# A decoder layer on one core: both ends laid out anew — the first phase in blocks of 256 tokens by two k-tiles, the last token tiles of 128 rows with the second half of the tokens completed first

## The chip, the cores and the metric

The kernel runs on one core of a Trainium2 chip. A core has five engines: TensorE (PE in the profile; PEld is its weight load), VectorE (DVE), ScalarE (ACT), GpSimd (POOL) and SyncE (SP), and here SP and POOL start the DMAs. The metric is the device time in microseconds of one execution; the figure given is the median of three.

## The reference

One step of a decoder layer on 512 new prompt tokens and 8 sample tokens, all in fp32; the model is 2048 wide. Half of the mixing is a gated delta rule with 8 heads of 128, half a pooling over trailing windows; a SwGLU layer 5632 wide follows, and a final norm.

```python
def decoder_layer(h, conv_buf, S0, pool_buf, start_pos, chunked, ...):
    xn = rmsnorm(h, norm_mix)
    proj = xn @ w_in                      # q | k | v | z | beta | decay | pool
    ...
    qkv_c, new_conv = short_conv(conv_buf, qkv, conv_w)       # 4 taps, then silu
    ...
    q = l2norm(q) * (DN_HEAD_DIM ** -0.5)
    k = l2norm(k)
    beta = sigmoid(b_raw)
    g = -exp(a_log) * softplus(a_raw + dt_bias)
    o, S = gated_delta_chunked(q, k, v, g, beta, S0f)          # samples: token by token
    dn_out = rmsnorm(o, dn_norm) * silu(z)
    pool_out, new_pool = multiscale_pool(pool_buf, p, start_pos, w_pool, pool_scale)
    h = h + concatenate([dn_out, pool_out]) @ w_out
    gu = rmsnorm(h, norm_ffn) @ w_gate_up
    h = h + (silu(gu[..., :D_FF]) * gu[..., D_FF:]) @ w_down
    return h, S, new_conv, new_pool
...
y_prompt = rmsnorm(hp, norm_final)
y_sample = rmsnorm(hs, norm_final)
```

## The kernel before

The 520 tokens (8 samples first, then the prompt) lie along the free dimension, and the 2048 channels as 16 tiles (k-tiles) of 128 partitions: `xh` and `xl` hold the normed input, `mixa` and `mixb` the raw one (8 k-tiles each) and later other things. Every fp32 operand is cut in a high part (`hi`, rounded) and a low part (`lo`, what is left), and each product is three matmuls (`step`, L179 to L181): high weight by high and by low input, low weight by high input. The tokens are worked in two chunks, `CHUNKS`, of 264 (samples and 256 prompt tokens) and 256. A weight tile arrives as granules of 8 k-tiles (`granule`): a DMA on SP into `raw`, the high part on ScalarE (L146), the low part on VectorE (L148).

**First phase** (the pool `ph0`, L265 to L512), written out by hand: the order of the lines is the order on every engine. The prompt arrives as four tiles of 128 tokens (`load_x`), and the work is 16 `Block`s of one token tile by four k-tiles: `turn` transposes it on TensorE to PSUM (L318), `fetch` copies it to `mixa`/`mixb` (L321), `norm` multiplies the copy by norm weight and root, four operations of 128 columns (L326), `high` makes the high part on ScalarE (L330), `low` the low part, mostly on POOL (L333). The root of a token tile comes from square sums (L283, L285), a power on POOL (`pow_mhalf`, L227), a diagonal matrix (L296) and a matmul with ones that spreads it over the partitions (L298). Behind the blocks stand the products of the first two key tiles: `first` in full (2 chunks x 16 k-tiles x 3 matmuls = 96), of `second` the first 8 k-tiles of one chunk (24). At the end the raw input is stored in DRAM (`spill`) on SP.

**The input projection.** Behind it `qkv_tile` makes one tile of 128 columns after the other: `product`, eviction to `ext`, convolution, silu. The tile of head 1 takes over `second` at k-tile 8 of chunk 0: its remaining 72 matmuls stand there. `product` calls `weave.step()` after each k-tile: a planner that lays small work between the matmuls, by steps that are counted; on its second track stand first `gates` (the beta and decay columns), then `keys(h)`, each 16 steps after its tile was made, so a product that is absent here is 16 steps fewer. `gates` stores the cumulative sums of the decays in DRAM (`gcr_d`, a DMA on SP, L617); `decay(h)` reads a head's row back, spread over all partitions (`gcb`, L754), subtracts (L757) and takes the exponential; `keys(h)` makes k times k (L774) and k transposed (L777) in two PSUM banks and scales them on VectorE (L789, L791). The PSUM banks named `dn` are a ring of five (`pst`), those named `mm` one of three.

**The middle** (products of z, q, v, pool, output and gate/up projections) is the same in both kernels, row for row on TensorE.

**The tail.** `w_down` is multiplied in pairs of output tiles by Strassen-Winograd's seven products (`Pair`): raw quarters A11 to A22 are loaded, the sums S1 to S4 made on VectorE (L1246), each cut in high and low (L1217, L1218), and products M1 to M7 accumulate in a `dn` bank each (`multiply`, L1224 to L1226, 24 matmuls here); `combine` adds the results to the residual in `mixa`/`mixb`. The order of the seven is `FIRST` in all pairs, the last too:

```python
    FIRST = ("M1", "M2", "M4", "M7", "M6", "M5", "M3")
```

With it a pair completes its first half of the tokens last. As channels complete, `squares` (L1749) puts their squares into the sum `sq2`. `token_roots` (L1831, L1834) sums `sq2` over the partitions for some token tiles and takes the power on POOL. `tokens(t)` transposes a token tile back (L1846), scales it, half on ScalarE (L1849), half on VectorE (L1851), and stores every 1024 columns by a DMA on SP (L1854, L1856). There are five tiles of `NT` = 104 tokens; the first holds the 8 samples.

## Time and profile before

| | us |
|---|---|
| three runs | 2189.26, 2186.50, 2185.41 |
| median | 2186.50 |
| the profiled execution (one of the three) | 2189.26 |
| its span in the profile | 2187.3 |
| granted clock of TensorE, mean | 0.995 |

The span runs from the first to the last recorded instruction; 1.96 us of the execution's time lie around it. A row of the timeline gives start, duration, engine, line, operation, what it writes and reads, and in brackets how long the engine had been idle and what released it. TensorE's matmuls overlap, so what one costs is read from start to start. Of what the prediction does not show: the DMA engines are used between 20 and 70% in every one of the page's 40 slices.

### The profile page before, as it was taken

To read this page: it belongs to the slowest core of one execution; us is meant where nothing else is said; L and a number is where in the kernel's file an instruction comes from. 1 tells how busy PE (TensorE), PEld (TensorE's weight loads), DVE (VectorE), ACT (ScalarE), POOL (GpSimd) and SP (SyncE) were. 2 spreads that over 40 slices of the span, in tenths; PEclk is the share of its full clock that TensorE was granted. 3 is DMA by queue.
4 is the path that set the end of the run, shared out by engine and by line. 5 is a ranking of instruction groups with operands and counts; after the bars stand their busy time and mean duration, and the time that the engine had idled before them with its cause. 6 is when DMAs were issued, how large, how long until landed. Compare 5 with 4: busy or idle time off the path is not lost.

```text
span 2187.3 us, 42971 instructions
## 1 busy us (share of the span) xinstructions
PE 2143.5 (98%) x17815; PEld 2135.1 (98%) x17815; DVE 1731.4 (79%) x2518; ACT 955.6 (44%) x1491; POOL 465.5 (21%) x520
## 2 busy tenths in 40 slices
PE   5999999999999999999999999999999999999998
PEld 5999999999999999999999999999999999999997
DVE  6576566566489979988888888888877898887996
ACT  5434454343255544443433434434334444445554
POOL 4111011011022211323233233232012303003120
PEclk8999999999999999999999999999999999999999
DMA  6443233423535542545445545554446746337333
GB/s 201 131 103 106 77 89 96 110 68 82 140 103 159 154 137 85 160 138 169 144 142 160 155 138 157 151 151 141 127 145 184 242 110 204 113 109 240 96 106 109
DMA packets 444728, 297.03 MB, mean 136 GB/s; under 512 B 26548, under 2 KB 424653, under 8 KB 441189
## 3 DMA queue, kind: packets, MB, share of 16 engines
q1 hardware_dynamic: 426661, 225.13, 36.6%
q0 software_dynamic: 16880, 68.51, 9.7%
q8 instruction: 139, 2.28, 0.4%
q10 hardware_dynamic: 992, 0.66, 0.1%
q14 instruction: 56, 0.46, 0.1%
HBM read 251.47 MB, written 43.43 MB: 135 GB/s over the span
## 4 chain that ended last, share of the span: by engine, by line
PE 88%; DVE 4%; ACT 2%; issue 1%; DMA 1%; POOL 0%; SPq 0%; DVEq 0%; ACTq 0%; POOLq 0%
PE dn L1224 21%; PE dn L1225 21%; PE dn L1226 21%; PE mm L179 7%; PE mm L181 6%; PE mm L180 6%; DVE lo L1218 1%; PE dn L854 1%; DMA st<-a_d 1%; ACT hi L1217 1%; DVE raw L1246 0%; PE dn L1846 0%; PE dn L964 0%; PE dn L861 0%; PE dn L900 0%
## 5 line engine op out<-in xcount | busy, mean ns | idle before, releaser
L1217 ACT CAST hi<-raw 128x1024 fp32r<-128x1024 f32 (+1 forms) x424 | 429.9, 1028 | 408.6 <-DVE raw L1246 215.0
L1218 DVE TENSOR_TENSOR lo<-raw,hi 128x1024 fp32r<-128x1024 f32 (+1 forms) x424 | 529.5, 1269 | 91.7 <-ACT hi L1217 89.9
L179 PE MATMUL mm<-xh,hi 128*128 128x256 f32 (+1 forms) x1280 | 380.4, 297 | 0.6 <-ACT ccs L735 0.6
L180 PE MATMUL mm<-xl,hi 128*128 128x256 f32 (+1 forms) x1280 | 362.9, 284 | 1.9 <-DVE xl L333 1.8
L181 PE MATMUL mm<-xh,lo 128*128 128x256 f32 (+1 forms) x1280 | 363.2, 284 | 0.2 <-DVE lo L148 0.2
L180 PEld LDWEIGHTS mm<-xl,hi 128*128 128x128 f32 x1280 | 243.7, 190 | 2.3 <-issue 1.9
L179 PEld LDWEIGHTS mm<-xh,hi 128*128 128x128 f32 x1280 | 243.2, 190 | 1.4 <-ACT ccs L735 0.7
L181 PEld LDWEIGHTS mm<-xh,lo 128*128 128x128 f32 x1280 | 242.4, 189 | 0.4 <-DVE lo L148 0.4
L1246 DVE TENSOR_TENSOR raw<-raw 128x1024 f32<-128x1024 f32 (+1 forms) x132 | 177.1, 1342 | 2.2
L1226 PE MATMUL dn<-b21h,lo 128*128 128x260 f32 x628 | 177.9, 283 | 0.1
L1224 PE MATMUL dn<-b21h,hi 128*128 128x260 f32 x628 | 177.7, 283 | 0.0
L1225 PE MATMUL dn<-b21l,hi 128*128 128x260 f32 x628 | 177.3, 282 | 0.4 <-DVE b21l L1730 0.4
L1226 PE MATMUL dn<-b11h,lo 128*128 128x260 f32 x620 | 175.4, 283 | 0.0
L1224 PE MATMUL dn<-b11h,hi 128*128 128x260 f32 x620 | 175.4, 283 | 0.0
L1225 PE MATMUL dn<-b11l,hi 128*128 128x260 f32 x620 | 174.9, 282 | 0.0
L148 DVE TENSOR_TENSOR lo<-raw,hi 128x1024 fp32r<-128x1024 f32 (+1 forms) x86 | 102.6, 1197 | 75.2 <-ACT hi L146 74.9
L1224 PE MATMUL dn<-T1h,hi 128*128 128x260 f32 x564 | 160.2, 284 | 0.0
L1225 PE MATMUL dn<-T1l,hi 128*128 128x260 f32 x564 | 160.0, 284 | 0.0
L1226 PE MATMUL dn<-T1h,lo 128*128 128x260 f32 x564 | 159.0, 282 | 0.0
L1224 PE MATMUL dn<-B22h,hi 128*128 128x260 f32 x556 | 157.6, 283 | 0.0
L1225 PE MATMUL dn<-B22l,hi 128*128 128x260 f32 x556 | 157.2, 283 | 0.0
L1354 POOL TENSOR_TENSOR mixa<-mixa 128x520 f32<-128x520 f32 x22 | 50.8, 2309 | 499.9 <-DVE mixa L1348 499.9
(590 smaller groups left out, 6526.7 us busy)
## 6 DMA issues: line engine op xcount, KB each, us to landing
raw<-in_w_gate_up_dram SPq DMA_DIRECT2D x134, 512.0 KB
raw<-in_w_in_dram SPq DMA_DIRECT2D x80, 512.0 KB
a_d<-mixa POOLq DMA_DIRECT2D x22, 1040.0 KB, 5.5
mixb<-in_w_gate_up_dram SPq DMA_DIRECT2D x42, 512.0 KB
raw<-in_w_down_dram SPq DMA_DIRECT2D x48, 448.0 KB
raw<-in_w_out_dram SPq DMA_DIRECT2D x25, 512.0 KB
st<-a_d POOLq DMA_DIRECT2D x49, 260.0 KB, 6.6
raw<-in_w_down_dram SPq DMA_DIRECT2D x24, 512.0 KB
```

The lines of the kernel that those rows point to most:

```text
L148: dve.tensor_tensor(lo[:, :f], raw[:, :f], hi[:, :f].bitcast(F32), op=ALU.subtract)
L179: te.matmul(acc[ci], wh, hi[k][:, c0:c1], start=(k == 0), stop=False)
L180: te.matmul(acc[ci], wh, lo[k][:, c0:c1], start=False, stop=False)
L181: te.matmul(acc[ci], wl, hi[k][:, c0:c1], start=False, stop=(k == len(w) - 1))
L854: te.matmul(yp[:, ck(c)], xt_[:, ck(c)], cur[:, ck(c)], start=True, stop=True)
L1217: act.copy(hi, raw)
L1218: dve.tensor_tensor(lo, raw, hi.bitcast(F32), op=ALU.subtract)
L1224: te.matmul(acc, wh[:, k, :], xf[:, k, :], start=start and k == 0, stop=False)
L1225: te.matmul(acc, wh[:, k, :], xg[:, k, :], start=False, stop=False)
L1226: te.matmul(acc, wl[:, k, :], xf[:, k, :], start=False, stop=stop and k == wh.shape[1] - 1)
L1246: dve.tensor_tensor(r[name], r[a], r[b], op=op)
L1354: pool.tensor_tensor(q[:, 4:8:2, :], q[:, 1:4:2, :], q[:, 0:2, :], op=ALU.subtract)
```

## The change

**First phase.** A block is now one chunk of 256 prompt tokens (two token tiles) by two k-tiles; 16 of them, those of chunk 0 first. `norm` reads the transposed input out of PSUM instead of the fetched copy, in two operations of 256 columns; all low parts are VectorE's. The loads change order (norm weights, samples and tile 2 ahead of other parameters; weights between tiles 3 and 4), all square sums are made in halves, and a loop over 17 steps does per step: fetch of block i + 2, high part of block i + 1, norm of i + 2, low part of i + 1, transposes of i + 4, and the products of block i. `second` is multiplied in full there too (its last weight granule lies in `hi3`, `lo3`); both key tiles are evicted to `ext` in the phase; the raw input is stored by POOL's queue during the second chunk. `qkv_tile` of heads 0 and 1 has no product left.

**Tail.** The last pair is a `LastPair`: order `LASTLY`, its banks from the ring `mm`, its sums made after the cuts and written over raw quarters, and each half of each output tile squared and scaled where it completes. Token tiles are the four of 128 prompt tokens, the samples are handled by themselves (`sample_rows`). The roots of tiles 2 and 3 and the transposes of tile 2 stand inside the last product M4.

```diff
+    def to_columns(ext, t, ci, acc):
+        if ci == 0:
+            act.copy(ext[:, 3:3 + 256], acc[:, NB:264])
+            act.copy(ccs[:, :, t], acc[:, 0:NB])
+        else:
+            act.copy(ext[:, 3 + 256:3 + 512], acc)
...
+            def norm(self, n=None):
+
+                if not n:
+                    self.xm = ph0.tile([P, 2, 256], F32, name="xm", bufs=4)
+                c = slice(0, 256) if n is None else slice(P * n, P * n + P)
+                r = slice(self.cols.start + c.start, self.cols.start + c.stop)
+                for kk in range(2):
+                    dve.scalar_tensor_tensor(self.xm[:, kk, c], self.pt[:, 256 * kk + c.start:256 * kk + c.stop],
+                                             nmix(self.k + kk), rb[:, r], op0=ALU.mult, op1=ALU.mult)
...
+        load_x(1)
+        sp.dma_start(pr0, norm_mix[0].rearrange("(t p) -> t p", p=P))
+        sp.dma_start(xts[0], x_sample.rearrange("b s (k p) -> (b s k) p", p=P))
+        load_x(2)
+        sp.dma_start(pr1[96:112, :], norm_ffn[0].rearrange("(t p) -> t p", p=P))
+        sp.dma_start(pr1[0:96, :], conv_w[0].rearrange("i (t p) -> (i t) p", p=P))
+        parts[0][0]()
+        load_x(3)
+        parts[1][0]()
+        load_x(4)
+        parts[2][0]()
+        sp.dma_start(wba_raw, w_in[0].rearrange("(k p) c -> p k c", p=P)[:, :, 4096:4112])
+        sp.dma_start(raw3.rearrange("p (k c) -> p k c", k=HG), win_view(1024 + P)[:, HG:2 * HG, :])
...
+            pool.dma_start(xs_d[4 * kg:4 * kg + 4].rearrange("k p c -> p k c"), m[:, r, :])
...
+        for i in range(17):
+            if i + 2 < 16:
+                B[i + 2].fetch()
+            if i + 1 < 16:
+                B[i + 1].high()
+            if i < 4:
+                square_sums(3 + i // 2, act, half[i % 2], i % 2)
+            if i == 1:
+                parts[1][1](act)
+            if i == 3:
+                parts[2][1](act)
+            if i == 6:
+                act.copy(hi3, raw3)
+            if i in (2, 4):
+                roots(2 + i // 2, 2)
+            if i in (4, 6):
+                on_all(1 + i // 2, pbs[1 + i // 2])
+            if i + 2 < 16:
+                B[i + 2].norm()
+            if i + 1 < 16:
+                B[i + 1].low()
+            if i in (2, 4):
+                dgs[2 + i // 2] = diagonal(2 + i // 2)
+                parts[i // 2][1](dve)
+            if i == 6:
+                dve.tensor_tensor(lo3, raw3, hi3.bitcast(F32), op=ALU.subtract)
             if i + 4 < 16:
                 B[i + 4].turn()
+            if i in (3, 5):
+                pbs[(i + 3) // 2] = spread(dgs[(i + 3) // 2])
+            ci, j = divmod(i, 8)
+            if i < 16:
+                first(ci, j)
+            if i == 7:
+                to_columns(ext_first, H, 0, acc_first[0])
+            if i in (9, 11, 13, 15):
+                spill((i - 9) // 2)
+            if 5 <= i < 13:
+                second(0, i - 5)
+            if i == 12:
+                to_columns(ext_second, H + 1, 0, acc_second[0])
+            if i == 15:
+                to_columns(ext_first, H, 1, acc_first[1])
+            if 12 <= i < 16:
+                second(1, i - 12)
+            if i == 16:
+                for j in range(4, 8):
+                    second(1, j)
...
-            if done < KT:
-                product(w or weights(win_view(sec * 1024 + h * P), KT), xhk, xlk, evict, acc, done)
-            else:
-                for ci, (c0, c1) in enumerate(CHUNKS):
-                    evict(ci, c0, c1, acc[ci])
+            if ext is None:
+                ext = columns()
+                product(weights(win_view(sec * 1024 + h * P), KT), xhk, xlk,
+                        lambda ci, c0, c1, acc: to_columns(ext, t, ci, acc))
...
-                         *{0: (w_first, acc_first, KT), 1: (w_second, acc_second, 8)}.get(h, ()))
+                         {0: ext_first, 1: ext_second}.get(h))
...
+    LASTLY = ("M1", "M7", "M6", "M5", "M3", "M2", "M4")
...
+        def take(self):
+            return ps_mm.tile([P, HALF], F32, tag="mm", name="mm")
+
+        def add(self, name):
+            r = self.raw
+            a, b, dst, op = {"S3": ("A11", "A21", "A21", ALU.subtract), "S2": ("A22", "S3", "S3", ALU.subtract),
+                             "S1": ("S2", "A11", "A11", ALU.add), "S4": ("A12", "S2", "S2", ALU.subtract)}[name]
+            r[name] = r[dst]
+            dve.tensor_tensor(r[name], r[a], r[b], op=op)
+
...
+            elif n == "M6":
+                add(u3, p)
+                add(u2, p, m1)
+                add(self.to(1, 1), u3)
+                add(self.to(1, 0), u3)
+            elif n == "M5":
+                add(self.to(1, 1), p)
+                self.done(1, 1)
+                add(u2, p)
+                add(self.to(0, 1), u2)
+            elif n == "M3":
+                add(self.to(0, 1), p)
+                self.done(0, 1)
+            elif n == "M2":
+                add(self.to(0, 0), p)
+                self.done(0, 0)
+            elif n == "M4":
+                add(self.to(1, 0), p)
+                self.done(1, 0)
...
+            lastly = isinstance(p4 or p, LastPair)
+            if name4 in ("S1", "S2", "S3") and not lastly:
                 p4.add(name4)
-            if name and name != "S4":
+            if name and (name != "S4" or lastly):
                 p.cut(name, pool_)
-            if name4 == "S4":
+            if name4 == "S4" or name4[:1] == "S" and lastly:
                 p4.add(name4)
             pairs[q].multiply(n)
             pairs[q].combine(n)
-            if name == "S4":
+            if name == "S4" and not lastly:
                 p.cut(name, pool_)
...
+        def done(i, half):
+
+            m, c = 2 * mp + i, slice(HALF * half, HALF * half + HALF)
+            add_up()
+            sq = wdp.tile([P, NTOK], F32, tag="sq", name="sq")[:, c]
+            act.activation(sq, mix[m][:, c], AF.Square)
+            act.activation(mix[m][:, c], mix[m][:, c], AF.Copy, scale=nfin(m))
+            dve.tensor_tensor(sq2[:, c], sq2[:, c], sq, op=ALU.add)
+
+        if part_ == len(SIZES) - 1 and mp == ORDER[-1]:
+            return LastPair(view, to, done)
...
+        for j in range(n):
+            pow_mhalf(rs[:, j:j + 1], sv[:, j:j + 1])
+            rv[tiles[j] if j < len(tiles) else "s"] = rs[:, j:j + 1]
...
+    def tokens(t, pairs=((2, 3), (1, 0))):
+
+        for pair in pairs:
+            ot = (fins[0][1] if fins else wpl).tile([P, HG * P], F32, tag="ot" if fins else "raw", name="ot")
+            for kg in pair:
+                pt = pst()
+                for kk in range(4):
+                    te.transpose(pt[:, kk * P:(kk + 1) * P], mix[4 * kg + kk][:, tile_(t)], ident)
+                o = ot[:, 512 * (kg % 2):512 * (kg % 2) + 512]
+                if kg % 2 == 0:
+                    act.activation(o, pt, AF.Copy, scale=rv[t])
+                else:
+                    dve.tensor_scalar(o, pt, rv[t], None, op0=ALU.mult)
...
-    def first_half():
-        squares(True)
-        rv.update(token_roots((0, 1)))
-        add_up(dve)
-
-    dps[-1][-1].between["M3"] = first_half
-    run(dps[-1][1:], r21s[1], sums)
+    lastp = dps[-1][-1]
+    lastp.between["M4"] = [(0, lambda: token_roots((2, 3))), (4, lambda: tokens(2))]
+    run(dps[-1][1:], r21s[1], sums, LASTLY)
     stage.pop()[0].close()
     for x in ("T4", "T3", "T2"):
         fls[x].close()
-    fins.append(stacked("fin"))
-    tokens(0, rv[0], (0, 1))
-    squares(True)
-    add_up(dve)
-
-    tokens(0, rv[0], (2, 3))
-    rv.update(token_roots((2, 3, 4)))
-    for t in range(1, 5):
-        tokens(t, rv[t])
+    fins.append(stacked("fin", 6))
+    tokens(3)
+    token_roots((0, 1), True)
+    tokens(0)
+    sample_rows()
+    tokens(1)
```

On ScalarE, in the first phase (`sq` is a square sum, L146 the high part of weights, `mixa`/`mixb` from `dn` a fetch, `xh` from `xm` a high part). Before:

```order
L321 COPY mixa<-dn 128x4x128
L330 CAST xh<-xm 128x4x128
L321 COPY mixb<-dn 128x4x128
L330 CAST xh<-xm 128x4x128
L321 COPY mixb<-dn 128x4x128
L283 ACTIVATE sq_289,ss_128<-xt_135 128x2048
L146 CAST hi<-raw 128x1024
L330 CAST xh<-xm 128x4x128 x2
L449 CAST xh<-xms 128x16x8
L330 CAST xh<-xm 128x4x128
L146 CAST hi<-raw 128x1024
```

After, behind the first high part of weights:

```order
L343 COPY mixa<-dn 128x2x256
L356 CAST xh<-xm 128x2x256
L456 CAST xh<-xms 128x16x8
L343 COPY mixa<-dn 128x2x256 x2
L356 CAST xh<-xm 128x2x256
L300 ACTIVATE sq_264,ss_133<-xt_140 128x1024
L343 COPY mixa<-dn 128x2x256
L356 CAST xh<-xm 128x2x256
L300 ACTIVATE sq_283,ss_133<-xt_140 128x1024
L146 CAST hi<-raw 128x1024
L343 COPY mixb<-dn 128x2x256
L356 CAST xh<-xm 128x2x256
```

Fetches and high parts ran in groups of one to three and square sums over 2048 columns stood between them; now a fetch, a high part and one piece of 1024 columns take turns.

On VectorE, at the first keys of the input projection (`dm` is the decay difference, `gcb` the row read back from DRAM, `kd` and `mixb` what `keys` makes). Before:

```order
L785 TENSOR_TENSOR sck<-sck,btok 128x4
L787 TENSOR_TENSOR sck<-sck,edec 128x4
L791 TENSOR_TENSOR kd<-dn,sck 128x512
L148 TENSOR_TENSOR lo<-raw,hi 128x1024
L757 SCALAR_TENSOR_TENSOR dm<-gcb,gcs,mneg 128x128 x4
L148 TENSOR_TENSOR lo<-raw,hi 128x1024
L757 SCALAR_TENSOR_TENSOR dm<-gcb,gcs,mneg 128x128 x4
L745 TENSOR_SCALAR y<-ext,prm 128x512
L789 SCALAR_TENSOR_TENSOR mixb<-dn,sck,dm 128x128 x8
```

After:

```order
L627 COPY gr<-dn 8x512
L620 TENSOR_SCALAR negc<-negc 128x32
L634 TENSOR_TENSOR sc_g_743<-sc_aq,ident 8x128
L640 COPY sgb<-dn 128x128
L148 TENSOR_TENSOR lo<-raw,hi 128x1024
L744 TENSOR_SCALAR y<-ext,prm 128x512
L779 TENSOR_SCALAR ss<-ss 128x4
L746 SCALAR_TENSOR_TENSOR y<-ext,prm,y 128x512
L756 SCALAR_TENSOR_TENSOR dm<-gcb,gcs,mneg 128x128 x4
L783 TENSOR_TENSOR sck<-rr 128x4
L785 TENSOR_TENSOR sck<-ss,rr 128x4
L746 SCALAR_TENSOR_TENSOR y<-ext,prm,y 128x512
```

The cumulative sums that are stored, `gr`, stand 22 rows ahead of the first `dm` before, with both first keys' `kd` between them; now they stand 8 rows ahead of it, and the first key's results (`mixb` by L788, `kd` by L790) follow it within ten rows.

On TensorE, the end of the last pair (`B22` the tokens' side of M3, `T4` that of M4; `sq` and `sqs` the sums of squares; `ident` marks transposes). Before, the end of the last product M3 and what follows:

```order
L1225 MATMUL dn<-B22l,hi 128x260
L1226 MATMUL dn<-B22h,lo 128x260
L1846 MATMUL dn<-ident,mixa 104x128 x8
L1846 MATMUL dn<-ident,mixb 104x128 x8
L1831 MATMUL dn<-ones,sq_23798 104x2 x3
L1846 MATMUL dn<-ident,mixa 104x128 x8
L1846 MATMUL dn<-ident,mixb 104x128 x8
```

After, the middle of the last product M4:

```order
L1226 MATMUL mm<-T4l,hi 128x260
L1227 MATMUL mm<-T4h,lo 128x260
L1925 MATMUL dn<-ident,mixb 128x128 x8
L1925 MATMUL dn<-ident,mixa 128x128 x8
L1225 MATMUL mm<-T4h,hi 128x260
L1226 MATMUL mm<-T4l,hi 128x260
```

and its end:

```order
L1226 MATMUL mm<-T4l,hi 128x260
L1227 MATMUL mm<-T4h,lo 128x260
L1925 MATMUL dn<-ident,mixb 128x128 x8
L1925 MATMUL dn<-ident,mixa 128x128 x8
L1904 MATMUL dn<-ones,sq_23789 128x2 x2
L1909 MATMUL dn<-ones,sqs 128x2
L1925 MATMUL dn<-ident,mixb 128x128 x8
L1925 MATMUL dn<-ident,mixa 128x128 x8
L1939 MATMUL dn<-ident,xs 128x128
L1925 MATMUL dn<-ident,mixb 128x128 x8
```

Before, all transposes stand behind the last product, the roots of tiles 0 and 1 in the middle of M3 and those of the other three behind the first tile's transposes; now the roots of tiles 2 and 3 stand ahead of M4, tile 2's 16 transposes in the middle of it and tile 3's right behind it, and the samples' tile is a transpose of its own.

More of the change, by code (lines that the diff above doesn't have):

```diff
@@ L392, in decoder_kernel @@
-        B[3].turn()
-        B[2].fetch()
+        dve.tensor_copy(prm[:, 96:112], ptp[:, 0:KT])
         sb = ph0.tile([P, P], F32, name="sb", bufs=1)
         dve.tensor_scalar(sb, ones, ss0[:, 0:1], None, op0=ALU.mult)
-        B[0].norm()
-        roots(2)
         pb = pst()
         te.matmul(pb[:, :NB], sb, sel, start=True, stop=True)
+        for h in range(2):
+            act.copy((mixa, mixb)[h][:, :, 0:NB],
+                     pt0[:, 0:P].rearrange("p (b k) -> p k b", k=KT)[:, 8 * h:8 * h + 8, :])
@@ L401, in decoder_kernel @@
         dve.tensor_scalar(rb[:, 0:NB], pb[:, :NB], 1.0 / D, EPS, op0=ALU.mult, op1=ALU.add)
         pow_mhalf(rb[:, 0:NB], rb[:, 0:NB])
-        B[3].fetch()
-        pt0 = pst()
-        te.transpose(pt0[:, 0:P], xts[0], ident)
-        B[4].turn()
-        B[1].norm()
-        B[0].high()
-        for half in range(2):
-            act.copy((mixa, mixb)[half][:, :, 0:NB],
-                     pt0[:, 0:P].rearrange("p (b k) -> p k b", k=KT)[:, 8 * half:8 * half + 8, :])
-        B[5].turn()
@@ L453, in decoder_kernel @@
+        B[0].low()
         dve.tensor_tensor(xl[:, :, 0:NB], xms, xh[:, :, 0:NB].bitcast(F32), op=ALU.subtract)
[L454 to L470 removed]
@@ L471, in decoder_kernel @@
-        B[12].turn()
-        first(0, 4, 8)
-        parts[2][1](act)
-        B[11].fetch()
-        B[9].high()
-        pb4 = spread(4)
-        B[13].turn()
-        B[8].low(pool)
-        parts[2][1](dve)
-        rows(4, pb4)
-        B[9].low(pool)
-        first(0, 8, 12)
-        B[12].fetch()
-        B[13].fetch()
-        first(0, 12, 16)
-        for i in range(10, 19):
-            if i < 16:
-                B[i].norm()
+        B[1].norm(1)
+        parts[0][1](dve, slice(2 * P, HG * P))
@@ L1167, in decoder_kernel @@
         mixed(0, 2)
+    pres.close()
     c1s.close()
```

328 lines of the change are left out of this document (141 added, 187 removed).

## The prediction

> **What bounds the kernel now.** I read the page first, then the list of waits of each engine, then the two ends row by row. Of the page:
>
> ```profile
> PE 2143.5 (98%) x17815; PEld 2135.1 (98%) x17815; DVE 1731.4 (79%) x2518; ACT 955.6 (44%) x1491; POOL 465.5 (21%) x520
> PE   5999999999999999999999999999999999999998
> ```
>
> TensorE is busy in 98% of the span and only the first and the last of the 40 slices fall short. So there are about 44 us to win, and both are at the ends. TensorE's waits once it runs are few:
>
> ```profile
> PE dn L298 <- DVE dg L296: 11.7, 3, 10.5
> PE dn L362 <- DMA pr<-in_conv_w_dram: 6.5, 1, 6.5
> PE dn L774 <- ACT mixb L748: 0.6, 1, 0.6
> ```
>
> (Columns: total wait in us, how often, the longest.) Both large ones belong to the first phase. Behind it nothing waits long, so what is saved at the head should travel through the dense middle to the end: the order of TensorE's rows is the same there in both kernels.
>
> **The first phase.** Rows of TensorE, then three stretches (busy us of PE, PEld, DVE, ACT, POOL, granted clock, DMA share, GB/s):
>
> ```profile
> 28.26 0.57 PE L179 MATMUL mm<-xh,hi 128*128 128x264 f32 x1
> 55.97 0.39 PE L179 MATMUL mm<-xh,hi 128*128 128x256 f32 x1 [0.58 <-ACT ccs L735]
> 8.00:10.00 2.00, 1.54 (x9) 1.14 (x7) 1.01 (x5) 1.11 (x3) 0.56 (x1) 1.00 0.98 383
> 20.00:25.00 5.00, 0.00 (x0) 0.00 (x0) 4.96 (x16) 2.20 (x5) 1.54 (x2) 0.54 0.41 96
> 38.00:40.00 2.00, 2.00 (x11) 2.00 (x10) 2.00 (x7) 0.00 (x0) 0.48 (x1) 0.50 0.59 227
> ```
>
> The first matmul of a product starts at 28.26 although the loads ran at 383 GB/s by 8; in 20 to 25 VectorE is busy 4.96 of 5 us and TensorE not at all. The prices:
>
> ```profile
> 37.21 0.28 PE L180 MATMUL mm<-xl,hi 128*128 128x264 f32 x1
> 37.33 0.28 PE L181 MATMUL mm<-xh,lo 128*128 128x264 f32 x1
> 38.07 0.42 PE L179 MATMUL mm<-xh,hi 128*128 128x264 f32 x1
> 38.29 0.42 PE L180 MATMUL mm<-xl,hi 128*128 128x264 f32 x1
> 40.92 0.28 PE L180 MATMUL mm<-xl,hi 128*128 128x264 f32 x1
> 36.65 0.60 PE L318 MATMUL dn<-ident,xt 128*128 128x128 f32 x4
> 37.01 0.37 PE L179 MATMUL mm<-xh,hi 128*128 128x264 f32 x1
> 5.65 1.06 ACT L283 ACTIVATE sq<-xt 128x1024 bf16<-128x1024 f32 x1 [3.55 <-DMA xt<-in_x_prompt_dram]
> 34.18 1.06 ACT L146 CAST hi<-raw 128x1024 fp32r<-128x1024 f32 x1
> 35.13 0.60 ACT L321 COPY mixa<-dn 128x512 f32<-128x512 f32 x1
> 35.60 0.64 ACT L330 CAST xh<-xm 128x512 fp32r<-128x512 f32 x1
> 36.12 0.61 ACT L321 COPY mixb<-dn 128x512 f32<-128x512 f32 x1
> 23.45 1.13 DVE L326 SCALAR_TENSOR_TENSOR xm<-mixb,prm,rb 128x128 f32<-128x128 f32 x4
> 17.12 3.15 DVE L326 SCALAR_TENSOR_TENSOR xm<-mixa,prm,rb 128x128 f32<-128x128 f32 x4 [0.98 <-POOL xl L333]
> 30.83 0.68 DVE L333 TENSOR_TENSOR xl<-xm,xh 128x512 fp32r<-128x512 f32 x1
> 80.77 0.75 DVE L747 SCALAR_TENSOR_TENSOR y<-ext,prm,y 128x512 f32<-128x512 f32 x1
> ```
>
> From start to start a product matmul costs 0.12 at full clock (37.21 to 37.33), 0.22 at half (38.07 to 38.29), and four transposes 0.36 (36.65 to 37.01). ScalarE pays 0.95 for 1024 columns (34.18 to 35.13), 0.47 to fetch 512 and 0.52 for their high part. On VectorE four norms of 128 columns take 1.13 alone and 3.15 while POOL subtracts. The new norms are of 256 columns out of PSUM, which no row shows: between 0.28 (1.13 / 4) and the 0.75 of a row of 512 columns I take 0.42, two to a block, 0.83, and 0.61 for the low part. With all low parts on VectorE, POOL has no long work left beside them, so the 3.15 should not recur.
>
> When would the product begin? x of tile 1 has landed by 5.65. Behind it come some 0.07 MB of samples, 1.05 MB of tile 2 and 0.52 MB of weights; at 383 GB/s they are there at about 9 and 10.5. The squares of tile 2 (halves on two engines, about 1.1) end at 10.1. Root, diagonal, spreading, norm and high part follow, about 4.9 with the hand-overs, and the first weights' high cut (0.95) lies among them: 15.0, against 28.26. The order of ScalarE's rows shows the block then being worked as fetch, high part, fetch.
>
> Blocks 0 to 4 are ScalarE's: two copies a block, 1.0, four half squares and three weight cuts of 0.95 among them, and with its waits on VectorE I count 2.6 a block: 15.0 + 5 x 2.6 = 28.0. Then TensorE has 192 - 30 = 162 product matmuls left, 162 x 0.12 = 19.4, and 11 times four transposes, 4.0: 51.4, with 0.3 for the evictions 51.7. VectorE needs 11 x 1.45 + 2 x 1.2 = 18.4 there and stays under it. Two stretches above were granted about half the clock, one with TensorE idle (0.54), one with it busy throughout (0.50); blocks 0 to 4 keep it near half busy, so I add 0.8 (eight matmuls x 0.10): end 52.5. Before, 72 of the 192 matmuls are still to come at 55.97: 72 x 0.12 = 8.6, equal work is done at 64.6. **Gain 12.1**, less 0.25 for the transposes of the parameters now at the phase's end. Bounds: 51 with no cold stretch; 57 where a norm out of PSUM costs 0.67, nearly the row of 512 columns (16 x 2 x 0.25 = 8 more on VectorE, of which about 5 would show).
>
> The Trainium skill (TensorE: Matmul & The Clock Gate, "Part 1: The HAM clock gate") says that TensorE falls to half rate after an idle window of about 3.4 us and comes back after as long a busy one. The row at 0.54, of an idle stretch, agrees. By that rule alone one return, not eight matmuls, would be paid: an estimate of 16 x 0.10 = 1.6.
>
> **The keys.** With 72 matmuls and 16 steps of weaving gone from the second key's tile, the chain of the gates moves against the keys' own rows:
>
> ```profile
> 85.11 0.97 PE dn L614 x8
> 86.82 0.30 SPq L617 DMA_DIRECT2D gcr_d<-gr  x1
> 102.83 0.53 SPq L754 DMA_DIRECT2D gcb<-gcr_d  x1
> 107.88 1.14 DVE L757 SCALAR_TENSOR_TENSOR dm<-gcb,gcs,mneg 128x128 f32<-128x128 f32 x4 [2.10 <-DMA gcb<-gcr_d]
> 109.34 2.15 DVE L789 SCALAR_TENSOR_TENSOR mixb<-dn,sck,dm 128x128 f32<-128x128 f32 x8
> 116.95 1.16 PE dn L774 x8
> ```
>
> Before, 32 us lie between the cumulative sums (85.11) and the last keys (116.95), and the round trip through DRAM (sums, store at 86.82; load at 102.83, landing before 107.88, 4.96 later) hides in them. Now the sums stand directly ahead of keys 0 to 2. Let X be the time of the sums: store at X + 1.7, load landing at X + 8 to 9.5, decay differences 1.14, exponential, then four of the eight rows at 109.34: key 0 leaves its PSUM bank at about X + 13. TensorE has only the sums (0.97), 48 product matmuls (5.8) and some two and a half keys (1.1 to 1.2 each, 3) to do until key 2, whose second bank is the one that key 0 still holds in the ring of five: it is there at about X + 10. So TensorE waits about 3.2 where it waited 0.6 (the row of L774 above): **-2.6**. Behind it queue the next tile's matmuls, and nothing else. Bounds: 0 (the store lands early) and 5 (the load two microseconds later, as its landings scatter).
>
> **The tail.** The last rows:
>
> ```profile
> 2140.00:2150.00 10.00, 10.00 (x86) 10.00 (x85) 9.24 (x14) 5.58 (x8) 0.00 (x0) 1.00 0.28 77
> 2165.60 1.18 POOL L227 TENSOR_TENSOR rv<-sv,mhalf 104x2 f32<-104x2 f32 x1 [33.12 <-DVE sv L1834]
> 2166.70 1.04 PE L1846 MATMUL dn<-ident,mixa 128*104 128x128 f32 x8
> 2167.40 0.69 ACT L1849 ACTIVATE ot<-dn,rv 104x512 f32<-104x512 f32 x1 [2.07 <-PE dn L1846]
> 2172.48 5.05 DVE L1851 TENSOR_SCALAR ot<-dn,rv 104x512 f32<-104x512 f32 x6 [0.19 <-PE dn L1846]
> 2170.00 11.79 SPq L1856 DMA_DIRECT2D out_dram<-ot  x9
> 2178.00:2179.00 1.00, 0.00 (x0) 0.00 (x0) 0.00 (x0) 0.00 (x0) 0.00 (x0) 1.00 0.85 307
> 2185.00:2186.00 1.00, 0.00 (x0) 0.00 (x0) 0.00 (x0) 0.00 (x0) 0.00 (x0) 0.50 0.23 94
> ```
>
> After 2178 every engine is done and only the store runs, at a share of 0.85 and 307 GB/s, until about 2185.35; the span ends 1.95 later. In the change the last pair starts at the same place and has the same seven blocks. I add 16 transposes of tile 2 inside its last block (two of the 1.04 rows overlapping, 1.75) and 1.4 for the squares of the half that completes late, which the roots at that block's head need: its last matmul ends at 2169.8 instead of 2166.7. Behind it stand three prompt tiles of four evictions each on two engines (0.69, and 5.05 / 6 = 0.84), three roots of 1.18 one after the other on POOL, the samples' 128 x 128: the last eviction ends near 2178.6. What is moved out earlier is tile 2's megabyte and half of tile 3's, so the store no longer queues; the last 0.52 MB needs 0.6 to start, 1.7 to move at 307 GB/s with 0.5 of latency, 1.95 to the end: 2183.4 against 2187.3, 3.8. The four sums of raw weights now stand behind the cuts of an engine busy 9.24 of 10 us, so an operand may be late: 0.5 off. **Gain 3.3**, bounds 0 (every operand late by half a microsecond and the samples' root last) and 5 (the store never waits).
>
> The Trainium skill (DMA: Bandwidth & Descriptors, the section on why a DMA increments its semaphore by 16, "How many engines") says that a transfer uses the largest number up to 16 that divides its rows: 104 rows give 13 engines, 128 give 16. 13 / 16 is 0.81 and the row at 2178 shows 0.85, so the trace nearly agrees. By the rule the last store would move in 13/16 of 1.7, an estimate of 0.3 less; the sum does not use it.
>
> **Sum.** 12.1 - 0.25 - 2.6 + 3.3 = 12.55. The profiled execution took 2189.26 (span 2187.3), which makes 2176.7; it is the slowest of three, the median 2186.5 makes **2174.0**.
>
> **The rivals.** *All of it*: the store lands early, no key waits, the tail gives 5: 12.1 - 0.25 + 0.6 + 5 = 17.5, 2169. For it: before, the same trip through DRAM was hidden entirely behind other rows. Against: the bank is asked for 3 us too soon. *Half of it*: norms out of PSUM cost 0.67 and the keys wait 5: 7.6 - 0.25 - 4.4 + 3.3 = 6.3, 2180. For it: VectorE was the bound in 20 to 25. *No change*: the early start is taken back by something tied to time and not to TensorE, such as the weights' loads; then only what the tail gives and a little more stays, 2184 to 2187. Against: no wait on a weight load stands in the list. *Slower*: the blocks feed TensorE in bursts and the granted clock stays near 0.5 through the phase. Then 192 x 0.22 + 16 x 0.60 = 51.8 from 15.0, plus 3.4 of waits in blocks 0 to 4, ends at 70.2, 5.6 behind 64.6; with -2.6 - 0.25 + 3.3 it is 5.2 slower, 2192. It decides once some 125 matmuls run at 0.22 (12.55 / 0.10). For it: 0.50 in 38 to 40 with TensorE busy in all of it. Against: that stretch was over at 40.92, where a matmul takes 0.28 again instead of 0.42, and from block 5 on TensorE is loaded fully.
>
> **The numbers.** Forecast 0.55, all of it 0.13, half 0.16, no change 0.07, slower 0.09. A measurement here tells 0.2%, 4.4 us, from no change: faster is the first three, 0.84, same 0.07, slower 0.09. The range, 2168 to 2184, holds the first three with the bounds of the terms; the forecast's own is 2170 to 2178.
>
> **What would show it.** The first product matmul at 14 to 17; TensorE without a gap from about 28; the phase's last product matmul near 52; VectorE's norm rows at about 0.4 each; a wait of 2 to 5 on the keys' bank; the last block ending 3 later than the seven blocks alone, and the store's end within 5 of the last eviction. It is wrong if the clock stays at half past 35, if the norm rows reach 0.7, or if the last pair's blocks show waits on VectorE of more than 2.

## The result, and the profile after

Four runs of the changed kernel take 2176.34 us in the median (2173.90 to 2177.61), four of the kernel before 2187.88 (2185.41 to 2189.63): 11.5 less, a ratio of 0.9947 with a 95% interval of 0.993 to 0.9964. Two later sets, each beside the kernel before on a chip of its own, give 0.9950 (0.9935 to 0.9965) and 0.9948 (0.9934 to 0.9962). It is faster, by 0.5%.

The profiled execution took 2173.90, its span 2172.2. The page's busy lines and slices of the changed kernel:

```profile
PE 2139.6 (99%) x17801; PEld 2131.8 (98%) x17801; DVE 1733.3 (80%) x2513; ACT 953.1 (44%) x1493; POOL 450.1 (21%) x515
PE   7999999999999999999999999999999999999998
PEclk9999999999999999999999999999999999999999
```

The first slice went from 5 to 7 tenths: that is the whole change as the page sees it. The larger waits of TensorE in the changed kernel (total, times, longest):

```profile
PE dn L416 <- DMA pr<-in_norm_mix_dram: 6.1, 1, 6.1
PE dn L1227 <- DVE lo L1219: 4.0, 4, 2.0
PE dn L318 <- DVE dg L313: 3.5, 3, 1.9
PE dn L776 <- DVE mixb L788: 1.8, 1, 1.8
PE dn L1904 <- DVE sq L1830: 1.6, 1, 1.6
PE mm L180 <- DVE xl L359: 1.3, 3, 0.7
```

The wait of 11.7 for the spreading matmuls is 3.5; two others have grown, at the third key (L776, 0.6 before) and ahead of the last product (L1904, 0.4 before). The four waits for low parts of weights (L1227) lie behind the first phase and were there before too, 3.4 in all; the prediction's list leaves that line out. TensorE's timeline at the places of the prediction's steps:

```profile
15.15 0.39 PE L179 MATMUL mm<-xh,hi 128*128 128x264 f32 x1 [0.90 <-ACT xh L456]
23.36 0.46 PE L318 MATMUL dn<-dg,ones 128*128 128x128 f32 x2 [1.86 <-DVE dg L313]
28.55 0.37 PE L179 MATMUL mm<-xh,hi 128*128 128x264 f32 x1
51.96 0.26 PE L516 MATMUL dn<-ident,pr 112*128 112x112 f32 x1
96.42 0.66 PE L776 MATMUL dn<-ident,mixb 128*128 128x128 f32 x4 [1.80 <-DVE mixb L788]
105.19 1.06 PE L773 MATMUL dn<-mixb 128*128 128x128 f32 x8
2153.44 0.61 PE L1904 MATMUL dn<-ones,sq 128*128 128x2 f32 x4 [1.60 <-DVE sq L1830]
```

The product begins at 15.15 (28.26 before), TensorE has no gap of note from 28.55, and the phase's last product matmul ends where the parameters' transpose starts, 51.96. The fourth keys start at 105.19 (116.95 before). From there to the last pair's first matmul, 2134.33, it is 2029.1; before, from 116.95 to 2146.10, 2029.2. The middle is untouched. The pair's begin to the span's end is 37.9 where it was 41.2. The store at the very end (windows: PE, PEld, DVE, ACT, POOL, clock, DMA share, GB/s):

```profile
2168.00:2169.00 1.00, 0.00 (x0) 0.00 (x0) 0.00 (x0) 0.00 (x0) 0.00 (x0) 1.00 1.03 414
2169.00:2170.00 1.00, 0.00 (x0) 0.00 (x0) 0.00 (x0) 0.00 (x0) 0.00 (x0) 0.93 0.99 393
2170.00:2171.00 1.00, 0.00 (x0) 0.00 (x0) 0.00 (x0) 0.00 (x0) 0.00 (x0) 0.50 0.36 139
```

With 128 rows the store moves some 400 GB/s at a share of 1.0, where 104 rows moved 307 at 0.85. It ends 2.7 behind the last eviction (2167.7) instead of 7.8 (2177.5 to 2185.35).

In these two profiled executions the spans differ by 15.1, not 11.5: the one of before was its second slowest of four, the one of the changed kernel its fastest. The experiments show most of the reason.

### The profile page after: what moved, and what is told of

It is laid out like the page before. It is cut to its first block, busy times and chain, and to the rows that moved or that the text cites. A ratio compares the mean times of both kernels' runs of the same rounds, so it can differ in the third digit from the quotient of the medians.

```text
span 2172.2 us, 42935 instructions
## 1 busy us (share of the span) xinstructions
PE 2139.6 (99%) x17801; PEld 2131.8 (98%) x17801; DVE 1733.3 (80%) x2513; ACT 953.1 (44%) x1493; POOL 450.1 (21%) x515
## 3 DMA queue, kind: packets, MB, share of 16 engines
q0 software_dynamic: 17968, 72.77, 10.3%
## 4 chain that ended last, share of the span: by engine, by line
PE 85%; DVE 8%; ACT 2%; DMA 2%; issue 1%; POOL 0%; DVEq 0%; ACTq 0%; POOLq 0%
PE dn L1225 19%; PE dn L1226 19%; PE dn L1227 19%; PE mm L179 7%; PE mm L180 7%; PE mm L181 7%; DVE lo L1219 3%; PE dn L853 1%; ACT hi L1218 1%; DVE raw L1247 1%; DMA raw<-in_w_down_dram 1%; DMA st<-a_d 1%; DVE mixb L1818 0%; PE dn L963 0%; DVE mixb L214 0%
## 5 line engine op out<-in xcount | busy, mean ns | idle before, releaser
L1219 DVE TENSOR_TENSOR lo<-raw,hi 128x1024 fp32r<-128x1024 f32 (+1 forms) x422 | 530.0, 1277 | 89.3 <-ACT hi L1218 87.9
L1227 PE MATMUL dn<-b21h,lo 128*128 128x260 f32 x620 | 175.6, 283 | 0.0
L1227 PE MATMUL dn<-b11h,lo 128*128 128x260 f32 x612 | 173.2, 283 | 0.0
L148 DVE TENSOR_TENSOR lo<-raw,hi 128x1024 fp32r<-128x1024 f32 (+2 forms) x86 | 101.6, 1185 | 85.5 <-ACT hi L146 85.0
L1227 PE MATMUL dn<-T1h,lo 128*128 128x260 f32 x556 | 156.7, 282 | 0.0
L1227 PE MATMUL dn<-B22h,lo 128*128 128x260 f32 x548 | 154.1, 281 | 0.4 <-DVE lo L1219 0.4
```

What stands on the lines that cost most here:

```text
L148: dve.tensor_tensor(lo[:, r], raw[:, r], hi[:, r].bitcast(F32), op=ALU.subtract)
L1219: dve.tensor_tensor(lo, raw, hi.bitcast(F32), op=ALU.subtract)
L1227: te.matmul(acc, wl[:, k, :], xf[:, k, :], start=False, stop=stop and k == wh.shape[1] - 1)
```

## The experiments

**The two ends alone.** The first kernel has the changed first phase and key tiles with the tail of before, the second the reverse. Both consist of parts of the diff above, nothing else:

```diff
 (the first phase, qkv_tile, keys)   after in the first kernel, before in the second
 (LastPair, roots, token tiles)      before in the first kernel, after in the second
```

> The changed first phase and key tiles with the tail of before. Theory (the two ends are separate terms): the product begins near 15, the phase's last product matmul ends near 52, the second bank of key 2 is waited for about 1.8, the last pair begins 11.8 earlier than before in the profile (2146.1 to about 2134.3), and from there on all is as before, 41.2 to the end of the span. The time falls by 8 to 12. Rival (one end alone carries the result, the other is worth nothing once it is there): the time is that of the whole change, 11.5 below before, or it is that of before.

> The changed last pair, roots and token tiles with the first phase of before. Theory: the last pair begins where it did (about 2146), waits 1.6 for the squares ahead of its last product, and the span ends 37.9 behind the pair's begin instead of 41.2: 3.3 less. Rival: the tail gains nothing by itself (0 +- 1), since the wait for the squares and the transposes inside the last product give back what the store saves; then the time is that of before.

Measured beside the kernel before (2188.48, 13 runs): head alone 2179.02, 9.5 less, ratio 0.9958 (0.9943 to 0.9972); tail alone 2185.83, 2.65 less, 0.9990 (0.9981 to 1.0000). Together 12.1, and the whole change has 11.5: the ends add up as separate terms. The head's gain is clear of the noise; the tail's is small, and its interval just reaches 1. Taken the other way, from each of the two kernels to the whole change on the same chip (2176.96, below), the head is worth 8.9 and the tail 2.1. Head alone waits its 1.80 at key 2 and starts the last pair at 2135.83, 10.3 earlier, not 11.8: its fourth keys come 0.5 later than in the whole change's profile, and the middle takes 1.0 more. Tail alone ends 37.4 behind its pair's begin, but its ten runs spread over 2182.7 to 2189.4.

**The spread.** The changed kernel once more.

> The changed kernel once more, for the spread of its runs. Its first profile showed a span 15.1 below that of before, the medians of four runs 11.5. Theory: single runs of either kernel scatter over some 4 us, before's profiled run was among its slowest and the changed one's its fastest; the stretch between the last keys and the last pair takes 2029 in each, and the new runs lie between 2173 and 2178. Rival: the middle became shorter with the change; then this profile shows the same 15 and the ratio moves to 0.993.

2176.96 (2175.40 to 2179.83), and this profile's span is 2175.6, 3.4 above the first one. One microsecond of it lies in the middle (the last pair begins at 2135.30). Of the other 2.4, in the tail, 0.6 is a wait for M3's PSUM bank that the first execution doesn't have; the rest the granted clock tells. Three stretches of 3.41 us, first in this execution, then in the first one. There the clock does not change at these places; its stretches are counted on in steps of 3.41 between its two changes at 19.47 and 2169.87:

```profile
2149.52:2152.93 3.41, 3.41 (x31) 3.41 (x30) 2.92 (x8) 0.81 (x2) 0.00 (x0) 1.00 0.02 5
2152.93:2156.34 3.41, 1.78 (x15) 1.57 (x15) 2.30 (x7) 1.77 (x5) 0.00 (x0) 1.00 0.00 0
2156.34:2159.75 3.41, 3.41 (x19) 3.41 (x18) 0.20 (x2) 0.81 (x2) 1.11 (x2) 0.50 0.00 0
```

```profile
2149.39:2152.80 3.41, 2.46 (x21) 2.25 (x19) 2.46 (x6) 1.23 (x3) 0.00 (x0) 1.00 0.02 5
2152.80:2156.21 3.41, 2.77 (x24) 2.77 (x25) 1.27 (x4) 1.65 (x5) 1.11 (x2) 1.00 0.00 0
2156.21:2159.62 3.41, 3.41 (x33) 3.41 (x31) 1.84 (x3) 1.62 (x3) 0.00 (x0) 1.00 0.40 161
```

The wait of 1.6 ahead of the last product is the same in both. Where it falls into one stretch (TensorE busy 1.78 of 3.41), the next stretch is granted half the clock and does 19 matmuls instead of 33. Where the border of two stretches cuts it (2.46 and 2.77), the clock stays. So the same wait costs 1.6 or some 3.3, and which of the two goes with where the border lies. Of the eleven profiled executions of this tail whose wait is 1.2 or more, seven show the half clock behind it, and their tails take 39.4 to 40.3 from the pair's begin, the other four 37.4 to 38.5. In the seven, TensorE was busy for 1.74 to 2.11 of the stretch with the wait; in the four, for 2.09 to 2.46 of the emptier one. The busy share alone does not decide it. The first profile's own wait of 1.80 at key 2 leaves a stretch emptier still, and the next one has the full clock:

```profile
94.56:97.97 3.41, 1.61 (x14) 1.55 (x14) 3.41 (x13) 2.57 (x6) 1.50 (x2) 1.00 0.24 67
97.97:101.39 3.42, 3.42 (x31) 3.42 (x30) 2.41 (x13) 3.33 (x7) 1.75 (x5) 1.00 0.41 86
```

Ten of the profiles have that wait of 1.8, and none shows a half stretch behind it. What else is needed, no run shows.

The first profile of before has two half stretches in its head:

```profile
37.48:40.90 3.42, 3.42 (x18) 3.42 (x17) 3.38 (x11) 0.50 (x2) 1.00 (x1) 0.50 0.62 236
51.14:54.55 3.41, 3.30 (x16) 3.01 (x15) 0.61 (x1) 0.00 (x0) 1.75 (x2) 0.50 1.03 288
```

The profile of the tail alone has the very same first phase without these two, and its third keys start 2.3 earlier. The rows of before, then of the tail alone:

```profile
103.40 1.05 PE L774 MATMUL dn<-mixb 128*128 128x128 f32 x8
101.07 1.05 PE L774 MATMUL dn<-mixb 128*128 128x128 f32 x8
```

That 2.3, and the 1.7 of half clock in the tail that the first profile of the changed kernel lacks, have the size of the 3.6 between 15.1 and 11.5; how many of the executions without a profile have either is not known. The expected rival, a shorter middle, is out.

The Trainium skill (TensorE: Matmul & The Clock Gate, "Part 1: The HAM clock gate") describes free-running windows of 3.4 us and the half rate after an idle one. The lengths agree. The traces show more: the half rate also came behind windows in which TensorE was busy for half of the time (1.78 of 3.41), and did not come behind others as empty (1.61).

**Key 2's wait.**

```diff
-                weave.add(keys(h), 1, 16)
+                weave.add(keys(h), 1, 24 if h == 2 else 16)
```

> The changed kernel with the third key's rows 8 weaving steps later (24 steps instead of 16 behind its tile), that is some 21 product matmuls or 2.5 us later on TensorE. Theory: TensorE's wait of 1.80 on key 0's rows disappears and nothing takes its place, so the fourth keys' row, at 105.2 in the changed kernel's profile, comes at about 103.4, and the time falls by 1.8. Rival: the chain of gates, decays and keys on VectorE and ScalarE sets the pace; then the wait moves to the third or fourth key's rows (a wait of 1 to 2 there) and the time stays.

2173.23 (2171.89 to 2176.51), ratio to before 0.9934 (0.9917 to 0.9951), against 2176.96 of the changed kernel on the same chip. Its key rows:

```profile
97.95 1.05 PE L773 MATMUL dn<-mixb 128*128 128x128 f32 x8
98.84 0.60 PE L776 MATMUL dn<-ident,mixb 128*128 128x128 f32 x4
103.96 1.05 PE L773 MATMUL dn<-mixb 128*128 128x128 f32 x8
```

No wait is left, and none has come in its place. Its phase ended 0.8 later than in the first profile (52.76), and the fourth keys start 1.2 earlier, so the stretch between is 2.0 shorter: the 1.8 and a little. The two medians differ by 3.7, more than the wait; the tails' clock would explain the rest, since this profile has no half stretch there, but only the rows of the keys show a cause. The wait is a cost of the change that eight steps of the planner take back.

**The second product between the blocks.**

```diff
-            if 5 <= i < 13:
-                second(0, i - 5)
...
+        for j in range(8):
+            second(0, j)
```

The same for chunk 1: all 96 matmuls stand behind the loop.

> The changed kernel with the second key tile's 96 matmuls not laid between the blocks but all behind the first one's. Same work. Theory (the second product fills TensorE while VectorE makes the blocks): with 6 matmuls a block TensorE needs 1.1 where VectorE needs 1.45, so the first product ends near 45.5, the 96 matmuls take 11.5 behind it, and the phase's last product matmul is at about 57 instead of 51.8: 5 later at the end too. Rival (TensorE is fed fully from block 5 on whatever the order): the phase ends at 52 and the time does not change.

2182.40, ratio 0.9972 (0.9959 to 0.9986): 6.0 below before instead of 11.5. TensorE's waits in that kernel (total, times, longest), and from its timeline the phase's end:

```profile
PE mm L180 <- DVE xl L359: 5.0, 9, 1.1
```

```profile
57.62 0.26 PE L512 MATMUL dn<-ident,pr 112*128 112x112 f32 x1
```

The phase ends at 57.6, 5.7 later, as expected: TensorE now waits for VectorE's low parts in nine places. About half of the head's gain is the second product as filling.

**Where the norm reads, and who makes the low parts.** Three kernels: the norm from ScalarE's copy in SBUF; every second block's low part on POOL; both.

```diff
-                    dve.scalar_tensor_tensor(self.xm[:, kk, c], self.pt[:, 256 * kk + c.start:256 * kk + c.stop],
+                    dve.scalar_tensor_tensor(self.xm[:, kk, c], self.raw[:, kk, c],
...
-                dve.tensor_tensor(self.lo, self.xm, self.hi.bitcast(F32), op=ALU.subtract)
+                (pool if self.k % 4 else dve).tensor_tensor(self.lo, self.xm, self.hi.bitcast(F32), op=ALU.subtract)
```

In the first and third the first two fetches stand ahead of their norms.

> The changed kernel with the norm read from ScalarE's copy in SBUF, as before, instead of from PSUM. Theory: an operation of 256 columns costs the same 0.40 from start to start out of either memory, and reading PSUM only takes the copy off the chain to the first blocks, about 0.5 a block while ScalarE sets the pace (blocks 0 to 4): the first product matmul comes 0.5 to 1 later, the phase ends 0.5 to 2 later. Rival: PSUM is the dearer source, an operation from SBUF takes 0.3, VectorE gains 16 x 2 x 0.1 = 3 and the phase ends 1 to 2 earlier.

> The changed kernel with the low part of every second block on POOL. Theory: VectorE's norm of 256 columns, 0.40 when POOL is quiet, takes two to three times as long while POOL subtracts, as the rows of 1.13 and 3.15 in the profile of before; half the blocks then cost VectorE 1 more and save it 0.6, POOL needs 1.5 to 2 for a low part and hands it on later, and the phase ends 3 to 6 later. Rival: POOL takes 8 x 0.6 off VectorE without hurting it, and the phase ends up to 1 earlier or, where TensorE is the bound, unchanged.

> The changed kernel with both: the norm read from ScalarE's copy in SBUF and the low part of every second block on POOL. With the norm out of PSUM, POOL's low parts (1.28 each) did not slow the norm rows at all (0.43 each while POOL subtracted). Theory (an operation of VectorE with both tensors in SBUF is held up while POOL runs one, and one with a tensor in PSUM is not): here the norm rows that meet a low part on POOL take 1 or more instead of 0.44, their mean over the phase rises from 0.48 to 0.6 or more, and the phase's last product matmul comes 2 to 5 later than with the norm from SBUF alone (52.6). Rival (the long rows of 3.15 in the profile of before had another cause, such as the order of the queue): the mean stays at 0.48 and the phase ends at 52.6 to 53.3.

The phase's end, by the transposes behind it, is 51.96 in the changed kernel, 53.00 with the norm from SBUF, 52.57 with POOL's low parts, 54.53 with both; the times are 2178.80, 2180.60 and 2180.05. The first came as expected: the first product matmul starts at 16.12, 1.0 later, and a norm costs the same out of either memory (mean 481 ns, 476 out of PSUM). The second expectation, 3 to 6 later, failed. VectorE's norm rows and POOL's low part beside them, in the kernel with PSUM norms:

```profile
35.48 1.72 DVE L352 SCALAR_TENSOR_TENSOR xm<-dn,prm,rb 128x256 f32<-128x256 f32 x4
35.82 1.31 POOL L359 TENSOR_TENSOR xl<-xm,xh 128x512 fp32r<-128x512 f32 x1 [2.97 <-ACT xh L356]
```

and in the kernel with both:

```profile
37.51 2.70 DVE L352 SCALAR_TENSOR_TENSOR xm<-mixa,prm,rb 128x256 f32<-128x256 f32 x4
37.71 1.42 POOL L359 TENSOR_TENSOR xl<-xm,xh 128x512 fp32r<-128x512 f32 x1 [3.33 <-ACT xh L356]
```

Four norms take 1.72 beside a low part when they read PSUM, 2.70 when both tensors lie in SBUF. The groups of VectorE over the phase (busy, mean ns of one), both edits first, then POOL's low parts alone:

```profile
L352 DVE SCALAR_TENSOR_TENSOR xm<-mixb,prm,rb 128x256 f32<-128x256 f32 x16 | 8.9, 599 | 1.4 <-ACT mixb L343 1.4
L352 DVE SCALAR_TENSOR_TENSOR xm<-mixa,prm,rb 128x256 f32<-128x256 f32 x12 | 8.1, 722 | 0.1
```

```profile
L352 DVE SCALAR_TENSOR_TENSOR xm<-dn,prm,rb 128x256 f32<-128x256 f32 x28 | 12.2, 478 | 3.4 <-ACT mixb L343 2.1 <-ACT mixa L343 0.6 <-DVE rb L322 0.5
```

With both edits the mean over the 28 norms is 652 ns, against 481 with the norm from SBUF alone and 478 with POOL's low parts alone: neither edit slows the norms by itself, both together do. The 3.15 for four norms before fits this, as a meeting of POOL with an operation whose two tensors are both in SBUF. The third kernel's phase came 1.5 later than the first's, less than the 2 expected. Of lows_pool's 4 us at the end only 0.6 arise in the phase; 1.2 are a wait for a load of the samples' pooling state, up to 73.55, that the changed kernel doesn't have, and some 2 lie in the middle, where executions of the changed kernel differ by up to 1.8; its cause stays open.

The Trainium skill (SBUF — State Buffer, "🔬 SBUF: two separate sides") says that VectorE and GpSimd share a pair of ports, held for a whole instruction by an operation of VectorE with two SBUF inputs or in a two-port mode. The rows of both kernels agree with it; beside the SBUF norms POOL's low parts are longer too (1.42 against 1.31 in the rows above).

**The tail's parts.** The roots of tiles 2 and 3 later; tile 2's transposes behind the last product.

```diff
-    lastp.between["M4"] = [(0, lambda: token_roots((2, 3))), (4, lambda: tokens(2))]
+    lastp.between["M4"] = [(3, lambda: token_roots((2, 3))), (4, lambda: tokens(2))]
...
-    lastp.between["M4"] = [(0, lambda: token_roots((2, 3))), (4, lambda: tokens(2))]
+    lastp.between["M4"] = [(0, lambda: token_roots((2, 3)))]
+    tokens(2)
     tokens(3)
```

> The changed kernel with the roots of tiles 2 and 3 after 3 of the 8 k-tiles of the last product instead of ahead of it. Theory: TensorE's wait of 1.60 for the squares is covered by nine matmuls (1.1) and falls to 0.5 or less; the last product ends 1.1 to 1.6 earlier and so does everything behind it. Rival: the end hangs on the store or on the evictions, which now wait for the roots; then the last product ends earlier and the span does not.

> The changed kernel with tile 2's transposes behind the last product instead of inside it. Theory (the chain from the last product over the squares, roots and evictions to the store sets the end, and the store has gaps, 0.29 and 0.62 busy in two of its microseconds): the last product ends 1.75 earlier, the roots of tiles 0 and 1 come by as much earlier, but the first store starts some 2 later and the store is then without gaps: the span's end behind the pair's begin is 37.9 - 1 to 37.9 + 0.5. Rival (the early transposes are what the new tail gains): it grows by 2 or more, to 40.

Roots later: 2175.43, ratio to before 0.9941 (0.9919 to 0.9964). The wait is 0.51, and from M2's last k-tile to the span's end it takes 19.7 (2153.97 to 2173.7) against 20.75 in the first profile: 1.0 better, just under the 1.1 to 1.6 expected, and the window with the wait keeps TensorE busy 2.90 of 3.41. From the pair's begin it is 37.6 against 37.9, as this execution also waits 0.58 for M3's bank. The time by itself does not tell it from the changed kernel: 0.9941 lies inside that one's interval (0.9935 to 0.9965). Transposes behind: 2177.11, the same as the changed kernel (0.9950 to 0.9948), pair's begin to the end 39.4, outside the 36.9 to 38.4 expected, with a half stretch of the clock in it; without that it would be some 37.7, an estimate (39.4 less the 1.7 above). Two profiles of the changed kernel with such a stretch take 40.3 and 39.6. The store starts some 3 later, counted from the pair's begin, and runs without a gap, share 1.00 to 1.05. No cost of where these transposes stand can be seen; the rival of 2 more fell.

**Put together.** Five edits: key 2 later and the roots later, as above; M3's PSUM bank from the ring of five; the spreading matmuls behind the block's product; the last token tile stored in four pieces.

```diff
-            if i in (3, 5):
-                pbs[(i + 3) // 2] = spread(dgs[(i + 3) // 2])
             ci, j = divmod(i, 8)
...
                 first(ci, j)
+            if i in (3, 5):
+                pbs[(i + 3) // 2] = spread(dgs[(i + 3) // 2])
...
         def take(self):
+            if "M5" in self.bank and "M3" not in self.bank and len(self.bank) == 4:
+                return pst()[:, :HALF]
...
+                if t == 1:
+                    sp.dma_start(y_prompt[0][P * t:P * t + P, 512 * kg:512 * (kg + 1)], o)
```

> The changed kernel with five small edits: the third key's rows 8 weaving steps later, the roots of tiles 2 and 3 after three k-tiles of the last product, M3's PSUM bank from the other ring, the two spreading matmuls of token tiles 3 and 4 behind the block's product instead of ahead of it, and the last token tile stored in four pieces of 512 columns. Theory: 1.8 from the keys, 1.0 from the roots, 0.5 from the bank, up to 0.5 from the spreading, 0.5 to 0.7 from the store: 4 to 4.5 below the changed kernel, about 2172. Rival: once the keys' wait is gone the others are hidden by the store and by VectorE: 2 to 2.5 below, about 2174.

> The changed kernel beside the last one on the same chip, to compare with. Expected at 2176.5 +- 1.

2173.56 (2172.44 to 2175.52, five runs) against 2177.52 (2175.75 to 2177.87) of the changed kernel on the same chip: 4.0 less; to before 0.9934 (0.9922 to 0.9947). The sum was right, its parts were not. The fourth keys come 2.1 earlier (1.8 expected). The spreading matmuls bring nothing: their wait falls from 3.5 to 0.5 and the one for low parts rises,

```profile
PE mm L180 <- DVE xl L359: 2.9, 5, 1.1
PE dn L1906 <- DVE sq L1832: 1.2, 1, 1.2
PE dn L318 <- DVE dg L313: 0.5, 1, 0.5
```

and the phase ends at 51.94. M3's bank is not waited for, where five of the other profiles wait 0.4 to 0.6, but the wait for the squares is 1.2 where the roots alone left 0.5: it is over 19.9 behind the pair's begin in both, since VectorE's chain ends when it ends. The finer store changes nothing (4.5 from the last eviction to the span's end in both). What the tail gained, 39.6 to 37.6, is mostly the half stretch of the clock that this profile doesn't have; the one that each of the two has in the middle, between 845 and 853, cancels.

## Why the prediction was right, point by point

- **The first product at 15.0** was at 15.15; blocks 0 to 4 took until 28.55 (28.0), and the phase ended at 51.96 (51.7 before the allowance for the clock, 52.5 with it). TensorE was granted half the clock once, in 16.06 to 19.47, while it was fed sparsely anyway.
- **The gain of 12.1** against the profile is 12.6, but the profile's own 64.6 held 2.3 of half clock that other executions don't have. Head alone gives 9.5 with the key's wait in it, so about 10.7 without: the term was some 1.5 too large because its base, 64.6, was taken from one execution.
- **A norm out of PSUM at 0.42** is 0.40 from start to start. That the 3.15 would not recur was right; the reason given, that POOL has no long work left, is not needed: it would not have recurred with POOL working.
- **The keys: a wait of 3.2** was 1.80. The place and the bank were right, and so was key 0's end (X is 82.8; its rows end at 96.3, X + 13.5, where 13 was forecast). TensorE arrived at X + 11.8, not X + 10: the sums are four groups of matmuls and not one, and each key is dearer than counted. The trip through DRAM was not what came last; the first difference started at 92.50 behind VectorE's convolution rows, not behind a landing.
- **The tail's 3.3** is exactly the difference of the two profiles (41.2 and 37.9), with the wait for the squares at 1.6 (1.4 forecast). That it comes out exact is the luck of this execution: with the half clock behind that wait, as in seven of eleven, the same tail takes 39.4 to 40.3 and gains 1 to 2. The step had no term for the clock; over ten runs the tail alone is worth 2.65.
- **The sum of 12.55** is 11.5: head 1.5 less, keys 1.4 more, tail 0.6 less, and the rest scatter. So the mechanisms were right, and the sum came nearer than its terms because their errors had opposite signs. None of the rivals came; the half clock that the slower one was built on appeared, but in single windows of 3.41 us and not throughout.

## What to carry to other kernels

Give a starved TensorE a second, independent product to fill the gaps between blocks: the same 96 matmuls are worth 5.7 us laid between them. Where POOL works, let VectorE's two-tensor operations read one of them from PSUM. And look at a wait of 1.5 us together with the granted clock behind it: its price can double by where a window's border falls, so a term read from one profiled execution can carry one or two such windows that the next one lacks.

## What the runs showed of the hardware that was not expected

The granted clock changes in whole windows of 3.41 us whose borders lie elsewhere in each execution; a window with TensorE busy for 1.78 of 3.41 was followed by one at half clock, at 0.22 us a matmul, with 2.46 and 2.77 not. But at key 2 a window with 1.61 was not followed by one either, so no threshold of the busy share comes out of these runs. It fits a good part of the spread of 4 to 7 us between executions of one kernel; no run set a border on purpose, and what decides stays open. And VectorE's rows with one tensor in PSUM ran at full pace beside POOL (0.43 each), while four of those with both in SBUF took 2.70 instead of 1.72.
